# A two-layer hybrid decoder trunk on one core: another order of the first loads, transposes and products

## The chip, the cores and the metric

The kernel runs on one core of a Trainium2 chip. The core has five engines that run side by side and wait for each other through semaphores: TensorE (PE, with its weight loads PEld) multiplies matrices and transposes blocks, VectorE (DVE) and ScalarE (ACT) work on elements, GpSimd (POOL) does small odd jobs, and SyncE (SP) mainly issues transfers. ScalarE and GpSimd can issue transfers too. The metric is the device time of one execution in microseconds (us), the median of several runs.

## The reference, cut to what matters

The program computes two decoder layers for 256 tokens of width 2048, in float32. Layer 0 mixes tokens with a causal softmax attention of 16 heads with forget gates, layer 1 with three dilated windows of 8 heads. Before each mixer and each MLP stands an RMS norm, and all results are added to one residual stream:

```python
def reference(x, fox_w_in, ...):
    for i in range(DEPTH):
        h = rms_norm(x, mix_norm_g[i])
        if i % N_MIXERS == 0:
            mix = fox_attention(h, fox_w_in[j], fox_b_f[j], fox_q_gain[j], fox_k_gain[j], fox_w_out[j])
        else:
            mix = dilated_attention(h, dil_w_in[j], dil_q_gain[j], dil_k_gain[j], dil_w_out[j])
        x = x + mix
        h = rms_norm(x, mlp_norm_g[i])
        x = x + sq_relu_mlp(h, mlp_w_up[i], mlp_w_down[i])
```

The change touches the beginning of layer 0: the load of `x`, its first norm and the products of the normed `x` with `fox_w_in`, whose columns are queries, keys, values and 16 gate columns. `fox_w_in` is 2048 x 6160.

## The kernel before

**Products.** Every large product has 2048 rows of contraction, cut into 16 steps of 128 rows (`KC`), and 512 columns (`NC`). To keep float32 accuracy with a single-pass format, both operands are split into a high and a low part in `float32r`, and each step makes three matmuls for each of the two token blocks: high by high, high by low, low by high (lines 339 to 341). A step is therefore six matmuls of 512 columns. The sums stand in two of four PSUM banks `acc` (`sums`, line 326) until a chain of smaller work has read them.

**Weights.** A list `plan` holds all weight tiles in order of use, each two row blocks of 128 by 512 columns, 512 KB. `load` brings the next one into one of five `raw` buffers, `split` casts it to `wh` on ScalarE (line 308) and subtracts to get `wl` on VectorE (line 309), five buffers each. In the steady state, a product that has used up a tile calls `split` for the tile five further on. When a tile is loaded, its transfer is issued on SP's queue, which is worked in order.

**The first norm.** `x` stands in four tiles `x0` to `x3` of 512 columns (both token blocks). The products need it transposed and scaled by the norm's gains: TensorE transposes blocks of 128 into PSUM (`ptx`, line 473, 32 of them), ScalarE scales and rounds to the high part (line 478), VectorE takes the low part (line 479); two steps of the contraction make a pair `hT`. The norm's factor `rstd` is applied after the products. It comes from the sums of squares (`junk`, line 489), which are done later. For the other three norms the same turn is made by VectorE in 32x32 blocks, written to DRAM with four transfers a tile and read back with one (`transposed_by_dma`, line 429).

**The order of work.** The order is written out by a small planner, `Jobs`. Each chain of small work is a generator that yields a number of steps to wait, or a key that another chain has to set. Each contraction step calls `jobs.tick()`. The scheduler below it keeps this order as priority on each engine and moves an instruction back where its inputs come later by its own estimate. `behind(...)` fixes that what follows is queued behind given instructions of the same engine; it is an order and not a wait.

**The start.** `warm` makes ScalarE load its table for Exp; eight transposes of `ident` run on TensorE (`wake`, line 116). `load_x(0)` and the first weight tile go out in halves on SP's and ScalarE's queues. The gains of the first norm come through GpSimd's queue (line 141), are transposed on TensorE and copied on VectorE (`gained`). The next seven transfers are held until then: `hold` (line 265) writes one column of each target tile on VectorE behind `gained`, and the transfer has to wait for that write.

```python
    for what in (load, lambda: load_x(1), load, lambda: load_x(2), load, lambda: load_x(3), load):
        what()
        issued["held"] = []
```

Then the products follow, for each of four head groups `j`: queries, keys, values. For `j == 0` the gates (`gate`, 32 matmuls into `pf`) stand between queries and keys.

**After the products.** `qk_chain` (line 512) squares the sums, takes the norm of each head, scales, turns the tiles in 32x32 blocks, writes them to DRAM on SP's queue and reads them back on GpSimd's (line 544), then scales and splits them. `fox_head` (line 705) waits for queries, keys, gate and mask, and makes the scores `sc_f` (line 623). `make_sel` (line 745) builds a selection matrix on GpSimd through a tile `self` (lines 747 and 749). These chains share five buffers with the tag `w`: squares, scaled queries and keys, `self`, `junk` and turned tiles.

`in_pair` (line 353), used so far at the beginning of the later layers' parts, runs two products in turn: the first 12 steps of both (`CUT`), then the last 4 of both.

Of the kernel before, what the change touches and what calls it, by code (L numbers as in the profile page):

```python
# [38 lines left out]
CUT = 12  # L39

# [48 lines left out]
def trunk(ctx: ExitStack, tc, x, fox_w_in, fox_b_f, fox_q_gain, fox_k_gain, fox_w_out, dil_w_in,  # L89
# [17 lines left out]
    nc.scalar.activation(warm, warm, AF.Exp)  # L107
# [3 lines left out]
    nc.gpsimd.memset(mhalf, -0.5)  # L111


    spare = ps_sc.tile([P, P], F32, tag="sc", name="spare")

    def wake(times):
        for _ in range(times):
            nc.tensor.transpose(spare, ident, ident)

    wake(8)  # L120
# [20 lines left out]
    mix_rows = gain_rows("g_mix", [mix_norm_g.rearrange(per_chunk, p=P)], nc.gpsimd)  # L141
# [79 lines left out]
    def add_pair(*chunks):  # L221

        for rows in ((0, CUT * P), (CUT * P, D)):
            for w, cols in chunks:
                add(w, rows, cols)
# [6 lines left out]
    for j in range(4):  # L232
        for part in range(3):
            add(fox_w_in[0], (0, D), [(part * D + j * NC, NC)])
# [39 lines left out]
    raws, splits = [], []  # L274

    def load():
# [6 lines left out]
        for c, width in cols:  # L283
            src = w[r:r + RAW_SUB * P, c:c + width].rearrange("(c p) n -> p c n", p=P)
            if i:
                with hold(t[:, 0, 0:1]):
                    issued["load"] = nc.sync.dma_start(t[:, :, at:at + width], src)
            else:

                for part, queue in enumerate((nc.sync, nc.scalar)):  # L290
                    queue.dma_start(t[:, part, at:at + width], src[:, part, :])
            at += width
# [3 lines left out]
    def split():  # L296
# [9 lines left out]
        with behind(*([issued["gained"]] if i == 0 else issued.get("n0", []) if i < 2 * W_BUFS else [])):  # L306
            for part in ([slice(0, 1), slice(1, 2)] if i < 1 else [slice(0, W_SUB)]):
                issued["cast"] = nc.scalar.copy(hi[:, part, :], raw[:, part, :])  # L308
                issued["cut"] = nc.vector.tensor_sub(lo[:, part, :], raw[:, part, :], hi[:, part, :].bitcast(F32))  # L309
        splits.append((hi, lo))  # L310
        state["split"] += 1
# [17 lines left out]
    def product_steps(acc, keys, lhs, steps):  # L329

        for k in steps:
# [4 lines left out]
            for t in range(NT):  # L336
                tok = slice(t * P, (t + 1) * P)
                first, last = k == 0, k == KC - 1
                nc.tensor.matmul(acc[t], ah[:, tok], hi, start=first, stop=False)  # L339
                nc.tensor.matmul(acc[t], ah[:, tok], lo, start=False, stop=False)  # L340
                issued["product"] = nc.tensor.matmul(acc[t], al[:, tok], hi, start=False, stop=last)  # L341
            if i == W_SUB - 1:
                used[0] += 1
                split()
# [8 lines left out]
    def in_pair(new, steps, posts):  # L353
# [75 lines left out]
    def transposed_by_dma(tag, col, n):  # L429
# [31 lines left out]
    def norm_chain(tag, col, n, ssp, wait, later):  # L461
        yield wait
        if tag != "n0":
            yield from transposed_by_dma(tag, col, n)
        else:
            for half in range(2):
# [9 lines left out]
                for i in range(2):  # L476
                    gc = gain[:, col + pr * 2 + i:col + pr * 2 + i + 1]
                    on_act = nc.scalar.activation(both[:, i, 0, :], pt[:, i, :], AF.Copy, scale=gc)
                    on_dve = nc.vector.scalar_tensor_tensor(both[:, i, 1, :], pt[:, i, :], gc,
                                                            both[:, i, 0, :].bitcast(F32), ALU.mult, ALU.subtract)  # L480
# [429 lines left out]
    first = normed("n0", 0, lambda n: (0, 2, 6, 10)[n], lambda n: (13, 11, 9, 7)[n])  # L910

    def load_x(n):
        for t in range(NT) if n == 0 else [slice(0, NT)]:
            with hold(xt[n][:, 0, 0:1]):
                queue = nc.scalar if t == 1 else nc.sync
                issued["load"] = queue.dma_start(xt[n][:, t, :], xv[:, t, n * NC:(n + 1) * NC])

    def rest():
        while state["split"] - used[0] < W_BUFS:
            split()  # L920
            yield 1

    load_x(0)
    load()
    gained = gain_columns("g_mix", mix_rows, 0)

    issued["gained"] = gained
    issued["held"] = True
    for what in (load, lambda: load_x(1), load, lambda: load_x(2), load, lambda: load_x(3), load):
        what()  # L930
        issued["held"] = []
    del issued["held"]
# [11 lines left out]
    for j in range(4):  # L944
        sel = make_sel(j)
# [3 lines left out]
        product(keys_h(tag), lhs_h(tag), lambda acc: qk_chain(  # L949
            acc, tag, ("fq", j), [(0, 2, FOX_G, qT[0]), (2 * P, 2, FOX_G, qT[1])]))  # L950
        if j == 0:
            jobs.need("wf")
            gate(tag)
        product(keys_h(tag), lhs_h(tag), lambda acc: qk_chain(
            acc, tag, ("fk", j), [(0, 2, FOX_G + 1, kT[0]), (2 * P, 2, FOX_G + 1, kT[1])]))
# [46 lines left out]
```

## Time and profile before

| What | Value |
|---|---|
| median of 3 runs | 2161.55 us (2160.7 to 2162.31) |
| profiled execution, own time | 2161.91 us |
| its span | 2160.2 us |
| TensorE busy | 2147.8 us (99%), 11208 instructions |
| VectorE, ScalarE, GpSimd busy | 1397.9, 1105.9, 74.1 us |
| DMA | 459.34 MB, 213 GB/s in the mean |
| first product matmul | 8.53 us after the span's start |

The span goes from the first to the last profiled instruction; the execution's own time holds what lies around it as well. The profile names an instruction by line, engine, what it writes and what it reads. Idle time of an engine is put down to whatever released it. Busy matmuls are pipelined, so TensorE's pace is read from the distance of their starts. In rows of stretches the columns are the stretch, its length, busy time and count of PE, PEld, DVE, ACT and POOL, the granted clock, the DMA engines' share and GB/s.

### The profile page before, as it was taken

To read this page: it belongs to the slowest core of one execution; us is meant where nothing else is said; L and a number is where in the kernel's file an instruction comes from. 1 tells how busy PE (TensorE), PEld (TensorE's weight loads), DVE (VectorE), ACT (ScalarE), POOL (GpSimd) and SP (SyncE) were. 2 spreads that over 40 slices of the span, in tenths; PEclk is the share of its full clock that TensorE was granted. 3 is DMA by queue.
4 is the path that set the end of the run, shared out by engine and by line. 5 is a ranking of instruction groups with operands and counts; after the bars stand their busy time and mean duration, and the time that the engine had idled before them with its cause. 6 is when DMAs were issued, how large, how long until landed. Compare 5 with 4: busy or idle time off the path is not lost.

```text
span 2160.2 us, 30057 instructions
## 1 busy us (share of the span) xinstructions
PE 2147.8 (99%) x11208; PEld 1912.6 (89%) x11208; DVE 1397.9 (65%) x1862; ACT 1105.9 (51%) x1545; POOL 74.1 (3%) x92
## 2 busy tenths in 40 slices
PE   9999999999999999999999999999999999999999
PEld 7888888988998998998888888888988988988988
DVE  6777787765655565566668777676655655655664
ACT  6565655644544454455555565546544543544442
POOL 1111000000000000000011010100000000000000
PEclk9999999999999999999999999999999999999999
DMA  7676667766666666667776776758666666666664
GB/s 251 220 225 196 224 201 233 248 203 204 199 203 205 200 201 204 203 199 241 244 242 207 232 226 195 259 177 275 215 204 201 200 204 204 198 203 204 202 210 144
DMA packets 292354, 459.34 MB, mean 213 GB/s; under 512 B 21944, under 2 KB 104432, under 8 KB 292208
## 3 DMA queue, kind: packets, MB, share of 16 engines
q1 hardware_dynamic: 288416, 446.27, 66.1%
q0 software_dynamic: 3232, 10.50, 1.4%
q8 instruction: 87, 1.43, 0.3%
q10 hardware_dynamic: 560, 0.66, 0.1%
q14 instruction: 59, 0.48, 0.1%
HBM read 438.48 MB, written 18.87 MB: 212 GB/s over the span
## 4 chain that ended last, share of the span: by engine, by line
PE 92%; DVE 3%; DMA 2%; issue 1%; ACT 1%; POOL 0%; SPq 0%; DVEq 0%; ACTq 0%; POOLq 0%
PE acc L340 19%; PE acc L341 19%; PE acc L339 19%; PE up_n1a_acc L403 5%; PE up_n3a_acc L403 5%; PE up_n3a_sc L403 3%; PE up_n1a_tp L403 3%; PE up_n1a_sc L403 3%; PE up_n3a_tp L403 3%; PE up_n3a_acc L407 3%; PE up_n1a_acc L407 3%; DMA raw<-in_dil_w_in_dram 2%; DVE wl L309 1%; PE up_n3a_tp L407 1%; PE up_n1a_sc L407 1%; PE up_n1a_tp L407 1%
## 5 line engine op out<-in xcount | busy, mean ns | idle before, releaser
L309 DVE TENSOR_TENSOR wl<-raw,wh 128x1024 fp32r<-128x1024 f32 (+1 forms) x801 | 975.0, 1221 | 686.7 <-ACT wh L308 681.0
L308 ACT CAST wh<-raw 128x1024 fp32r<-128x1024 f32 (+1 forms) x801 | 837.7, 1048 | 931.7 <-PE acc L341 567.4
L339 PE MATMUL acc<-wh,hT_n 128*128 128x512 f32 x896 | 343.0, 384 | 0.5 <-ACT wh L308 0.5
L340 PE MATMUL acc<-wl,hT_n 128*128 128x512 f32 x896 | 339.9, 379 | 0.1
L341 PE MATMUL acc<-wh,hT_n 128*128 128x512 f32 x896 | 339.5, 379 | 0.0
L339 PE MATMUL acc<-wh,aTh_n1a 128*128 128x512 f32 x512 | 194.0, 379 | 0.0
L340 PE MATMUL acc<-wl,aTh_n1a 128*128 128x512 f32 x512 | 194.0, 379 | 0.0
L341 PE MATMUL acc<-wh,aTl_n1a 128*128 128x512 f32 x512 | 194.0, 379 | 0.0
L341 PEld LDWEIGHTS acc<-wh,hT_n 128*128 128x128 f32 x896 | 169.3, 189 | 24.1
L339 PEld LDWEIGHTS acc<-wh,hT_n 128*128 128x128 f32 x896 | 169.6, 189 | 23.4 <-ACT wh L308 0.9
L340 PEld LDWEIGHTS acc<-wl,hT_n 128*128 128x128 f32 x896 | 169.8, 190 | 22.6 <-DVE wl L309 0.4
L339 PE MATMUL acc<-wh,aTh_n3a 128*128 128x512 f32 x480 | 181.9, 379 | 0.0
L340 PE MATMUL acc<-wl,aTh_n3a 128*128 128x512 f32 x480 | 181.9, 379 | 0.0
L341 PE MATMUL acc<-wh,aTl_n3a 128*128 128x512 f32 x480 | 181.9, 379 | 0.0
L403 PE MATMUL up_n1a_acc<-hT_n,wh 128*128 128x512 f32 x512 | 181.6, 382 | 0.0
L403 PE MATMUL up_n3a_acc<-hT_n,wh 128*128 128x512 f32 x512 | 181.6, 382 | 0.0
L407 PE MATMUL up_n1a_acc<-hT_n,wl 128*128 128x256 f32 x512 | 139.6, 273 | 0.0
L407 PE MATMUL up_n3a_acc<-hT_n,wl 128*128 128x256 f32 x512 | 139.6, 273 | 0.0
L341 PEld LDWEIGHTS acc<-wh,aTl_n1a 128*128 128x128 f32 x512 | 96.8, 189 | 13.8
L340 PEld LDWEIGHTS acc<-wl,aTh_n1a 128*128 128x128 f32 x512 | 96.8, 189 | 13.7
L339 PEld LDWEIGHTS acc<-wh,aTh_n1a 128*128 128x128 f32 x512 | 96.8, 189 | 13.6
L403 PEld LDWEIGHTS up_n3a_acc<-hT_n,wh 128*128 128x128 f32 x512 | 96.8, 189 | 13.5
(725 smaller groups left out, 3202.3 us busy)
## 6 DMA issues: line engine op xcount, KB each, us to landing
raw<-in_mlp_w_up_dram SPq DMA_DIRECT2D x256, 512.0 KB, 4.1
raw<-in_mlp_w_down_dram SPq DMA_DIRECT2D x256, 512.0 KB, 4.2
raw<-in_dil_w_in_dram SPq DMA_DIRECT2D x192, 256.0 KB, 4.6
raw<-in_fox_w_in_dram SPq DMA_DIRECT2D x95, 512.0 KB, 4.1
raw<-in_fox_w_out_dram SPq DMA_DIRECT2D x32, 512.0 KB, 4.3
raw<-in_dil_w_in_dram SPq DMA_DIRECT2D x32, 512.0 KB, 4.4
raw<-in_dil_w_out_dram SPq DMA_DIRECT2D x32, 512.0 KB, 4.4
blocks_n<-turned_n SPq DMA_DIRECT2D x96, 64.0 KB, 2.4
```

The source lines that it names most:

```text
L308: issued["cast"] = nc.scalar.copy(hi[:, part, :], raw[:, part, :])
L309: issued["cut"] = nc.vector.tensor_sub(lo[:, part, :], raw[:, part, :], hi[:, part, :].bitcast(F32))
L339: nc.tensor.matmul(acc[t], ah[:, tok], hi, start=first, stop=False)
L340: nc.tensor.matmul(acc[t], ah[:, tok], lo, start=False, stop=False)
L341: issued["product"] = nc.tensor.matmul(acc[t], al[:, tok], hi, start=False, stop=last)
L403: issued["product"] = nc.tensor.matmul(banks[b], hi[:, i, col], in_turn(tokens.rearrange("p x s -> p (x s)"), P // 2), start=first, stop=last)
L407: nc.tensor.matmul(banks[b][:, 0:S], lo[:, i, col], in_turn(tokens[:, 0, :], P // 2), start=False, stop=False)
```

## The change

- The gains of the first norm are issued by ScalarE's queue instead of GpSimd's. The table load for Exp follows behind ScalarE's second transfer.
- `wake` runs float32r matmuls of 512 columns on a tile of zeros (a buffer of tag `w`) instead of transposes of `ident`: six at first, and two behind the first transposes.
- The first transfers are half of `x0` (256 columns, both token blocks), the first row block of weight tile 0 on ScalarE's queue, the second on SP's, the other half of `x0`, then weight tile 1.
- Six more transfers (`x1`, tiles 2, 3, 4, `x2`, `x3`) each wait for a fill of their whole target tile by GpSimd; the fills are queued one behind the other.
- The first split is made in two row blocks; the second one is queued behind the first pair of hT. The hT operations and the next splits are queued behind each other in the written order, and `rest` makes its first split one step later.
- Queries and keys of group 0 are made with `in_pair`, cut at 8 steps; the gates stand between their two last parts, and the first `make_sel` behind the pair. The weight plan follows that order.
- `x2` and `x3` are transposed like in the later norms, through DRAM; the block writes go by SP's queue and the read by GpSimd's. The due times in steps of the four parts change.

```diff
+FIRST_CUT = 8
...
-    nc.scalar.activation(warm, warm, AF.Exp)
...
-    nc.gpsimd.memset(mhalf, -0.5)
-    spare = ps_sc.tile([P, P], F32, tag="sc", name="spare")
+    ready = nc.gpsimd.memset(mhalf, -0.5)
+    spare = ps_sc.tile([P, NC], F32, tag="sc", name="spare")
+    zeros = work.tile([P, NC], F32R, tag="w", name="zeros", bufs=5)
+    nc.vector.memset(zeros.bitcast(F32), 0.0)
     def wake(times):
         for _ in range(times):
-            nc.tensor.transpose(spare, ident, ident)
-    wake(8)
+            nc.tensor.matmul(spare, zeros[:, 0:P], zeros, start=True, stop=True)
+    wake(6)
...
-    mix_rows = gain_rows("g_mix", [mix_norm_g.rearrange(per_chunk, p=P)], nc.gpsimd)
+    mix_rows = gain_rows("g_mix", [mix_norm_g.rearrange(per_chunk, p=P)], nc.scalar)
...
     for j in range(4):
-        for part in range(3):
-            add(fox_w_in[0], (0, D), [(part * D + j * NC, NC)])
+        chunks = [(fox_w_in[0], [(part * D + j * NC, NC)]) for part in range(3)]
+        if j == 0:
+            add_pair(*chunks[0:2], cut=FIRST_CUT)
+        for w, cols in chunks[2 if j == 0 else 0:]:
+            add(w, (0, D), cols)
...
-    def hold(first):
+    def hold(whole):
         if "held" not in issued:
             return ExitStack()
-        with behind(issued["gained"]):
-            nc.vector.memset(first, 0.0)
-        return behind(*([issued["load"]] if issued["held"] == [] else []))
+        with behind(*issued["held"]):
+            issued["held"] = [nc.gpsimd.memset(whole, 0.0)]
+        return behind(issued["load"])
...
-        with behind(*([issued["gained"]] if i == 0 else issued.get("n0", []) if i < 2 * W_BUFS else [])):
-            for part in ([slice(0, 1), slice(1, 2)] if i < 1 else [slice(0, W_SUB)]):
-                issued["cast"] = nc.scalar.copy(hi[:, part, :], raw[:, part, :])
-                issued["cut"] = nc.vector.tensor_sub(lo[:, part, :], raw[:, part, :], hi[:, part, :].bitcast(F32))
+        with behind(*(issued.get("n0", []) if i < 2 * W_BUFS else [])):
+            issued["cast"] = nc.scalar.copy(hi, raw)
+            issued["cut"] = nc.vector.tensor_sub(lo, raw, hi.bitcast(F32))
         splits.append((hi, lo))
+        cuts.append(issued["cut"])
...
-                nc.tensor.matmul(acc[t], ah[:, tok], hi, start=first, stop=False)
+                with behind(*([issued["product"]] if first and 0 < used[0] < W_BUFS else [])):
+                    nc.tensor.matmul(acc[t], ah[:, tok], hi, start=first, stop=False)
...
-                split()
+                if state["split"] >= W_BUFS:
+                    split()
...
-    def in_pair(new, steps, posts):
+    def in_pair(new, steps, posts, cut=CUT, between=lambda: None):
         banks = []
         for n in range(2):
             banks.append(new(n))
-            steps(banks[n], range(CUT))
+            steps(banks[n], range(cut))
         for n in range(2):
-            steps(banks[n], range(CUT, KC))
+            steps(banks[n], range(cut, KC))
             jobs.spawn(posts[n](banks[n]))
+            if n == 0:
+                between()
...
-    def transposed_by_dma(tag, col, n):
+    def transposed_by_dma(tag, col, n, queue, steps, *order):
...
-            nc.vector.transpose(tile_.rearrange("p (j b r) -> p b j r", j=4, b=4),
-                                xt[n][:, t, :].rearrange("p (b j c) -> p b j c", j=4, c=32))
+            with behind(*order):
+                nc.vector.transpose(tile_.rearrange("p (j b r) -> p b j r", j=4, b=4),
+                                    xt[n][:, t, :].rearrange("p (b j c) -> p b j c", j=4, c=32))
...
-            nc.sync.dma_start(tile_, blocks.rearrange("j c i x -> (j c) (i x)"))
+            queue.dma_start(tile_, blocks.rearrange("j c i x -> (j c) (i x)"))
             tiles.append(tile_)
-        yield 9
+        yield steps
...
-            yield from transposed_by_dma(tag, col, n)
+            yield from transposed_by_dma(tag, col, n, nc.sync, 9)
+        elif n > 1:
+            yield from transposed_by_dma(tag, col, n, nc.gpsimd, 9 + n, cuts[n + 2], issued["n0"][1])
...
+                    with behind(*issued.get(tag, [])):
+                        on_act = nc.scalar.activation(both[:, i, 0, :], pt[:, i, :], AF.Copy, scale=gc)
+                        on_dve = nc.vector.scalar_tensor_tensor(both[:, i, 1, :], pt[:, i, :], gc,
+                                                                both[:, i, 0, :].bitcast(F32), ALU.mult, ALU.subtract)
+                    issued[tag] = on_act, on_dve
...
-    first = normed("n0", 0, lambda n: (0, 2, 6, 10)[n], lambda n: (13, 11, 9, 7)[n])
+    first = normed("n0", 0, lambda n: (0, 2, 4, 5)[n], lambda n: (8, 9, 4, 2)[n])
...
     def rest():
+        yield 1
         while state["split"] - used[0] < W_BUFS:
...
+    nc.sync.dma_start(*halves_x[0])
+    with behind(nc.scalar.dma_start(first_raw[:, 0, :], first_w[:, 0, :])):
+        nc.scalar.activation(warm, warm, AF.Exp)
+    with behind(nc.sync.dma_start(first_raw[:, 1, :], first_w[:, 1, :])):
+        issued["load"] = nc.sync.dma_start(*halves_x[1])
...
+    with behind(issued["load"]):
+        load()
+    issued["held"] = [ready]
+    for what in (lambda: load_x(1), load, load, load, lambda: load_x(2), lambda: load_x(3)):
         what()
...
+    split_row_block(0)
     jobs.spawn(first(0))
     with behind(issued["transposed"]):
-        wake(3)
-    split()
-    for n in range(1, NX):
+        wake(2)
+    with behind(*issued["n0"]):
+        split_row_block(1)
...
+    jobs.spawn(first(1))
+    jobs.spawn(rest())
+    for n in range(2, NX):
         jobs.spawn(first(n))
-    jobs.spawn(rest())
...
-        sel = make_sel(j)
+        sel = make_sel(j) if j else None
...
+        if j == 0:
+            in_pair(lambda n: sums(), lambda acc, ks: product_steps(acc, keys_h(tag), lhs_h(tag), ks),
+                    [q_post, k_post], FIRST_CUT, gates)
+            sel = make_sel(j)
+        else:
+            product(keys_h(tag), lhs_h(tag), q_post)
+            product(keys_h(tag), lhs_h(tag), k_post)
```

`gates` is the former call of `gate`, `q_post` and `k_post` are the former `qk_chain` calls, and `split_row_block` casts and subtracts one row block of tile 0 behind `gained`.

More of the change, by code (lines that the diff above doesn't have):

```diff
@@ L219, in add, with add_pair @@
             plan.append((w, r, cols))
-    def add_pair(*chunks):
-        for rows in ((0, CUT * P), (CUT * P, D)):
+    def add_pair(*chunks, cut=CUT):
+        for rows in ((0, cut * P), (cut * P, D)):
             for w, cols in chunks:
@@ L284, in load @@
             src = w[r:r + RAW_SUB * P, c:c + width].rearrange("(c p) n -> p c n", p=P)
[L285 to L291, printed above, removed]
+            with hold(t):
+                issued["load"] = nc.sync.dma_start(t[:, :, at:at + width], src)
             at += width
@@ L907, in normed @@
         return lambda n: norm_chain(tag, col, n, ssp, wait(n), later(n))
-    first = normed("n0", 0, lambda n: (0, 2, 6, 10)[n], lambda n: (13, 11, 9, 7)[n])
+    first = normed("n0", 0, lambda n: (0, 2, 4, 5)[n], lambda n: (8, 9, 4, 2)[n])
     def load_x(n):
[L913 to L916, printed above, removed]
+        with hold(xt[n]):
+            issued["load"] = nc.sync.dma_start(xt[n], xv[:, :, n * NC:(n + 1) * NC])
     def rest():
+        yield 1
         while state["split"] - used[0] < W_BUFS:
```

36 lines of the change are left out of this document (21 added, 15 removed).

## The prediction

> **What bounds the kernel now.** I read the page's first part, then the list of who waited for whom on TensorE, then the busy time by stretches, and last the timeline of the first 20 us.
>
> ```profile
> span 2160.2 us, 30057 instructions
> ...
> PE 2147.8 (99%) x11208; PEld 1912.6 (89%) x11208; DVE 1397.9 (65%) x1862; ACT 1105.9 (51%) x1545; POOL 74.1 (3%) x92
> ```
> ```profile
> PE spare L118 <- POOL ident masks.py:199: 2.5, 1, 2.5
> PE ps_g_mix L137 <- DMA g_mix<-in_mix_norm_g_dram: 2.1, 1, 2.1
> ...
> PE sc_f L623 <- ACT fkT_0h L560: 1.1, 1, 1.1
> ...
> PE acc L339 <- ACT wh L308: 0.5, 1, 0.5
> ```
> ```profile
> 0.00:8.53 8.53, 3.88 (x16) 3.10 (x16) 2.00 (x12) 3.10 (x5) 4.89 (x16) 1.00 0.46 128
> 8.53:15.58 7.05, 6.44 (x31) 5.04 (x31) 3.54 (x7) 3.77 (x7) 0.00 (x0) 1.00 0.99 325
> 15.58:23.02 7.44, 7.44 (x41) 6.55 (x40) 5.50 (x8) 5.02 (x10) 0.00 (x0) 1.00 1.05 389
> ...
> 85.25:87.75 2.50, 1.26 (x7) 0.86 (x6) 1.99 (x3) 2.50 (x6) 0.00 (x0) 1.00 0.20 46
> ```
> ```profile
> 8.53:15.58 7.05, 5.62 (x18) 3.60 (x19) 0.00 (x0) 0.00 (x0) 1.00 0.99 325
> 15.58:23.02 7.44, 7.05 (x30) 5.61 (x31) 0.00 (x0) 0.00 (x0) 1.00 1.05 389
> ```
> ```profile
> 15.39 0.44 PE ptx_n L473 x4
> 15.83 0.22 PE acc L339
> ```
>
> The reader is to see that TensorE is the bound nearly everywhere. The four waits shown, 6.2 us together (2.5, 2.1, 1.1 and 0.5), all lie in the first 88 us. The third fence is busy time by stretches (PE, weight loads, DVE, ACT, POOL), the fourth the same for the matrix products into `acc` alone, the fifth two rows of the chain that ended last. A product matmul costs 0.22 us, a step of the contraction has six of them (1.3 us), a transpose of a 128x128 block costs 0.44/4 = 0.11 us. So 8.53 to 15.58 holds three steps, 18 x 0.216 = 3.9 us, and 12 transposes, 1.3 us: 5.2 us of work in 7.05 us, 1.9 us lost. The next 7.44 us hold five steps, 6.5 us, and 8 transposes, 0.9 us: nothing is lost there. What can be won is therefore the start (8.53 us before the first product), the 1.9 us after it, PE work that is taken away, and the wait of the first attention head at 85 us. The rest of the kernel only shifts.
>
> **The change part by part.** The start of before, from the timeline:
>
> ```profile
> 0.81 0.42 ACTq L916 DMA_DIRECT2D x<-in_x_dram  x1
> 1.42 0.66 POOL L130 DMA_DIRECT2D g_mix<-in_mix_norm_g_dram  x1 [0.33 <-issue]
> 2.43 0.54 POOL L747 MEMSET self<- 128x512 f32 x1
> 6.19 1.14 ACT L308 CAST wh<-raw 128x512 fp32r<-128x512 f32 x2 [3.43 <-DMA raw<-in_fox_w_in_dram]
> 6.62 0.31 PE L137 MATMUL ps_g_mix<-ident,g_mix 32*128 32x32 f32 x1 [2.11 <-DMA g_mix<-in_mix_norm_g_dram]
> 6.86 1.11 PE L473 MATMUL ptx_n<-ident,x 128*128 128x128 f32 x4
> 7.20 0.38 SPq L287 DMA_DIRECT2D raw<-in_fox_w_in_dram  x1
> 8.01 0.47 ACT L478 ACTIVATE hT_n<-ptx_n,gain 128x256 fp32r<-128x256 f32 x1 [0.68 <-PE ptx_n L473]
> 8.53 0.80 PE L339 MATMUL acc<-wh,hT_n 128*128 128x512 f32 x1
> 9.03 0.47 ACT L478 ACTIVATE hT_n<-ptx_n,gain 128x256 fp32r<-128x256 f32 x1 [0.55 <-DVE hT_n L479]
> 9.54 0.48 DVE L479 SCALAR_TENSOR_TENSOR hT_n<-ptx_n,gain,hT_n 128x256 fp32r<-128x256 f32 x1 [0.54 <-ACT hT_n L478]
> 9.97 0.38 PE L340 MATMUL acc<-wl,hT_n 128*128 128x512 f32 x1
> 10.19 0.59 PE L341 MATMUL acc<-wh,hT_n 128*128 128x512 f32 x2
> 11.91 1.04 ACT L308 CAST wh<-raw 128x1024 fp32r<-128x1024 f32 x1 [0.17 <-DMA raw<-in_fox_w_in_dram]
> 12.98 1.23 DVE L309 TENSOR_TENSOR wl<-raw,wh 128x1024 fp32r<-128x1024 f32 x1 [0.73 <-ACT wh L308]
> 15.65 1.23 DVE L309 TENSOR_TENSOR wl<-raw,wh 128x1024 fp32r<-128x1024 f32 x1 [0.48 <-ACT wh L308]
> 18.35 1.22 DVE L309 TENSOR_TENSOR wl<-raw,wh 128x1024 fp32r<-128x1024 f32 x1 [0.69 <-ACT wh L308]
> ```
> ```profile
> x<-in_x_dram ACTq DMA_DIRECT2D x1, 256.0 KB, 4.0
> turned_n<-blocks_n SPq DMA_DIRECT2D x24, 256.0 KB, 2.9
> qn_('fq', 0)_1_576<-blocks_('fq', 0)_1_586 POOLq DMA_DIRECT2D x1, 256.0 KB, 5.8
> ```
>
> *First loads and gains.* In before the gains, issued by GpSimd at 1.42, hold the transposes until 6.62. Now ScalarE issues them first, at 0.81, and they are 16 KB: they cannot be later than the 256 KB which the same queue brought in 4.0 us, at 4.8. The half of x that the first two steps need is 256 KB at the head of SP's queue: 4.8 us by the same row. Row block 0 of the weights stands second on ScalarE's queue behind 16 KB. It lands between 4.8 and the 6.2 us at which before had all of its first 1 MB; I take 5.1. Its cast is 1.14/2 = 0.57 us, so it is done at 5.7. From the first transpose to the first product before took 8.53 - 6.86 = 1.67 us, hence the first product starts at 4.85 + 1.67 = 6.5 us (7.2 if the row block comes at 6.2; 6.1 if the transposes run at full pace).
>
> *From the first product to the fourth step.* The second row block is now cast behind the second hT operation of ScalarE. By the rows 8.53, 9.03 and 9.54, that operation begins 0.5 us after the first product and its VectorE partner ends at +1.5; the cast ends at +1.55, the subtraction of 0.69 at +2.2, while the first step's six matmuls end at +1.3 to +2.0. Then four transposes (+0.45), hT on ScalarE, VectorE, ScalarE (three times 0.5), which ends at about +3.8, then raw1's cast, which stands behind them in the new order: 1.04, to +4.8. Step 2 starts there, its low part after the subtraction of 1.23 at +6.0, and step 3 starts at +6.5, with all 16 remaining transposes done: 13.0 us. Before started that step at 15.58 with the same 16 done. Gain 2.6 us. In before, raw1, issued at 7.20 behind the gains, was the late one (cast at 11.91, the wait of 0.5); now it is sent right after x's second half without a wait, is there by about 8 us, and ScalarE's order is what comes last.
>
> *Transposes of x2 and x3.* 16 of 32 leave TensorE: 16 x 0.11 = 1.7 us. The first two products in pair give them time: x2 is needed only at the ninth step of the first product, after 16 steps of work, at about 13.0 + 13 x 1.3 = 29.8 us.
>
> *Idle float32r matmuls.* Six of 512 columns on zeros from about 1.3 us, two more behind the first transposes. They run beside the loads and cost nothing. The first four products of before stood nearly 0.5 us apart (8.53 to 9.97), the next two 0.22: at least 0.8 us lost at half pace, though the granted clock reads 1.00 throughout. The wait on `ident` disappears too, and nothing hangs on it. If TensorE is at full pace from 4.8 us on, 1.3 us are won (0.4 on the transposes, so that the first product comes at 6.1, and 0.8 or a little more on the products); if the pace comes as late as before, nothing. I take 0.4. [...]
>
> *Fills on GpSimd.* Six fills of 128x1024, 1.1 us each (0.54 for 512 columns), so loads go out about as fast as 390 GB/s can take them (512 KB in 1.35 us); raw1 to raw4, x2 and x3 then land one after the other until about 15 us, 5 us ahead of before. TensorE eats one in 2.6 us. Cost nothing; were the loads late, each would cost its own delay, as raw1's did.
>
> *The pace of the splits.* Before, subtraction followed subtraction in 2.7 us (12.98, 15.65, 18.35) with a pair of hT in between, and TensorE needs 2.6 for two steps. With the new order behind hT, a chain by hand gives 3.25 us (1.23 + 0.5 + 0.5 + 0.5 + 1.04, less some overlap): two times 0.7. Between 0 and 1.4 I take 0.4, nearer to the measured pace.
>
> *x2 through DRAM.* Its turning on VectorE stands behind raw4's subtraction, at about 20 us by the same count.
>
> ```profile
> 51.62 1.80 SPq L543 DMA_DIRECT2D blocks_('fq', 0)_0_579<-sq_('fq', 0)_0_525  x4
> 53.52 1.85 SPq L543 DMA_DIRECT2D blocks_('fq', 0)_1_586<-sq_('fq', 0)_1_527  x4
> 57.40 0.55 POOL L544 DMA_DIRECT2D qn_('fq', 0)_1_576<-blocks_('fq', 0)_1_586  x1 [1.46 <-DMA blocks_('fq', 0)_1_586<-sq_('fq', 0)_1_527]
> 73.19 0.53 POOL L747 MEMSET self<- 128x512 f32 x1 [8.08 <-DVE fqT_1l L562]
> 73.80 2.54 POOL L749 TENSOR_SCALAR_AFFINE_SELECT self<-self 128x512 f32<-128x512 f32 x2
> 76.29 0.60 POOL L544 DMA_DIRECT2D qn_('fk', 0)_0_771<-blocks_('fk', 0)_0_777  x1
> ```
>
> The same path for the queries took 51.62 to 57.40 + 5.8 = 63.2, 11.6 us. From 20.7 that is 32.3, against a need at 29.8 for the first token half and 30.5 for the second: up to 1.8 us of wait. With SP's 2.9 us for the same read it would be 29.4 and no wait. The eight block writes, 3.65 us of SP's time for each x tile, stand ahead of raw loads, which have 5 us in hand; GpSimd's queue is empty there. Half of the measured excess, lessened by products that can run on the first half: 0.5.
>
> *The head's wait at 85 us* (1.1 us, 1.3 with its latency). TensorE waits for the keys, whose read GpSimd issued at 76.29 behind `self` of the next group, which had waited 8 us for the last reader of a query tile. Counted in steps of the job list, the query chain started at step 19, where `rstd` is due in before, and the key chain at 32; now the query product ends at step 24 and the key product still at 32, so the queries are five steps later against the keys, and `make_sel(0)` stands between them. If `self` of the next group falls behind the keys' reads, 3.1 us are won and the wait is gone; if the queries' later release holds the keys, it grows (rival 3). I take -0.6, half of the wait.
>
> Sum: -2.6 - 1.7 - 0.4 + 0.4 + 0.5 - 0.6 = -4.4 us on 2160.2 of span. The profiled run's own time was 2161.91, the median 2161.55, so they stand within 0.4 us; 2161.55 - 4.4 = 2157.1, by 0.20%. 0.2%, 4.3 us, is about what a measurement of this kernel can tell from no change.
>
> **The rivals.**
>
> 1. *The start is won and the splits and x2 give it back.* Both upper ends: +1.0 for the pace and +1.3 for x2, the head's wait unchanged, +0.6: -1.5, so 2160.0. For it: the new order on ScalarE, and 5.8 us for GpSimd's reads. Against it: the 2.7 us pace. [...]
>
> 2. *The start doesn't come earlier.* Row block 0 shares the 16 DMA engines with x's halves and raw1 and comes with the whole first megabyte at 6.2: first product 7.2, step 3 at 13.7, and no pace won. That leaves -1.9 - 1.7 + 0.9 - 0.6 = -3.3: 2158.2.
>
> 3. *The keys come late for the first heads, and it ends slower.* The `w` tiles are five. The query chain holds three of them; `self` takes the next one free and 3.1 us of GpSimd; the keys' tiles follow. With the queries released 5 steps (6.5 us) later against the keys' product, the keys are 6.5 + 3.1 = 9.6 us later and the wait of 1.3 becomes 10.9: -4.4 + 0.6 + 9.6 = +5.8, 2167.3. It is slower from 3.8 us of growth on, by over 0.2% from 8.1 on. Against it: the written order of TensorE's work can put products ahead of that head.
>
> **How the numbers follow.** The sum as it stands, or better, 0.50: faster by over 0.2%, predicted 2156.7, midway between the sum (2157.1) and what full pace from the start gives (2156.2). Rival 1, 0.28, and rival 2, 0.10, both within 0.2%. Rival 3, 0.12, of which 0.10 slower by over 0.2% and 0.02 within. So 0.50, 0.40, 0.10. Range: below, all good ends (full pace -1.3 in place of -0.4, pace and x2 free, -0.9, no head wait, -0.7): -6.9, 2154.6. Above, rivals 1 and 2 whole and the small case of rival 3: 2161.8.
>
> **What would show it.** The first product at 6.1 to 7.2 us (8.53 before); matmuls 0.22 apart from the first step on if the pace is full; step 3 at 13.0; 16 `ptx` transposes in place of 32; no stretch with idle TensorE at 30 us; the wait of `sc_f` near 81 us gone or as before. Wrong if the first product isn't ahead of 7.5 us, if TensorE waits over 2 us for hT of x2, or if a wait of `sc_f` above 3 us stands in the list.

## The result and the profile after

The changed kernel takes 2182.22 us (median; 2182.05 to 2183.47) against 2161.55 us: a ratio of 1.0098, 95% interval 1.0087 to 1.0108. It is 20.7 us slower. The forecast was 2156.7 us, with a range up to 2161.8 us.

The first rows of the page, and then the list of who waited for whom on TensorE (us in total, times, longest), of the changed kernel:

```profile
span 2180.5 us, 30075 instructions
...
PE 2152.5 (99%) x11189; PEld 1914.7 (88%) x11189; DVE 1402.4 (64%) x1868; ACT 1107.5 (51%) x1553; POOL 80.4 (4%) x101
```
```profile
PE acc L341 <- ACT hT_n L459: 8.8, 1, 8.8
PE sc_f L633 <- ACT fkT_0h L570: 3.4, 1, 3.4
PE ps_g_qk L139 <- DMA g_qk<-in_dil_k_gain_dram: 3.0, 1, 3.0
PE sc_f L630 <- ACT fkT_0w L563: 2.2, 1, 2.2
PE acc L341 <- ACT hT_n L487: 1.7, 1, 1.7
```

The wait on `g_mix` is gone. In its place stand longer ones, and all three signs of being wrong that the prediction named are there: a first product behind 7.5 us, over 2 us of wait for hT of `x2`, and over 3 us for `sc_f`. Line 459 is hT made from `x2` and `x3`, the parts that come back from DRAM. It costs most. Lines 630 and 633 are the scores of the first heads, 5.6 us where before had 1.1. `g_qk` is a small constant that TensorE transposes, in its written order, ahead of that hT product. TensorE's busy time rose too, by 4.7 us, although there are 19 instructions fewer. The stretches show why. Columns: stretch, length, busy time and count of PE, PEld, DVE, ACT and POOL, granted clock, DMA share, GB/s.

```profile
5.90:7.62 1.72, 0.05 (x1) 0.00 (x0) 0.39 (x1) 0.99 (x2) 0.88 (x1) 1.00 1.01 369
7.62:8.50 0.88, 0.88 (x3) 0.51 (x4) 0.69 (x2) 0.15 (x1) 0.00 (x0) 1.00 1.06 410
8.50:10.00 1.50, 1.50 (x4) 1.17 (x5) 1.12 (x2) 0.83 (x2) 0.00 (x0) 0.50 1.06 408
10.00:11.50 1.50, 1.50 (x7) 1.26 (x6) 0.06 (x1) 0.26 (x1) 0.00 (x0) 0.50 1.05 385
...
34.00:38.30 4.30, 0.25 (x2) 0.22 (x2) 0.56 (x2) 0.00 (x0) 2.18 (x7) 1.00 0.55 168
38.30:47.20 8.90, 0.16 (x1) 0.05 (x1) 4.50 (x11) 5.21 (x11) 0.06 (x1) 0.55 0.99 347
47.20:50.00 2.80, 2.77 (x7) 2.20 (x8) 1.94 (x7) 2.80 (x8) 0.00 (x0) 0.50 1.03 349
50.00:52.40 2.40, 2.40 (x7) 1.95 (x6) 2.40 (x6) 2.26 (x8) 0.00 (x0) 0.50 0.49 158
53.00:60.00 7.00, 7.00 (x34) 6.14 (x33) 4.11 (x10) 6.42 (x15) 0.53 (x1) 1.00 0.56 169
```

TensorE stands nearly still from 33.8 to 47.2 us, and after it the clock is granted at 0.50 for 5.2 us: seven matmuls in 2.8 us, where full pace makes 34 in 7.0.

The starts of the contraction steps, counted from 0 and read from the timelines, place the loss (us after the span's start):

| step | before | changed | later by |
|---|---|---|---|
| 0 (first product) | 8.53 | 7.62 | -0.9 |
| 3 | 15.59 | 16.31 | +0.7 |
| 15 | 32.97 | 32.51 | -0.5 |
| 24 (behind the gates in both) | 49.37 | 64.10 | +14.7 |
| 50 | 83.97 | 99.09 | +15.1 |
| 54 (behind the first head) | 91.64 | 112.70 | +21.1 |

So the loss has two places: 15.2 us between steps 15 and 24, and 5.9 us at the first heads. From there on the two kernels run in parallel, and the spans end 20.3 us apart.

**The first place.** Three queues meet there. SP's queue, then ScalarE, then the product that waited (timeline of the changed kernel):

```profile
22.91 10.61 SPq L445 DMA_DIRECT2D blocks_n<-turned_n  x16
33.57 0.48 SPq L166 DMA_DIRECT2D bf<-in_fox_b_f_dram  x1
34.09 0.32 SPq L132 DMA_DIRECT2D g_qk<-in_fox_q_gain_dram  x1
...
36.29 27.36 SPq L292 DMA_DIRECT2D raw<-in_fox_w_in_dram  x13
```
```profile
25.37 1.05 ACT L308 CAST wh<-raw 128x1024 fp32r<-128x1024 f32 x1 [1.72 <-DMA raw<-in_fox_w_in_dram]
...
41.63 1.04 ACT L308 CAST wh<-raw 128x1024 fp32r<-128x1024 f32 x1 [15.21 <-DMA raw<-in_fox_w_in_dram]
...
45.24 1.03 ACT L308 CAST wh<-raw 128x1024 fp32r<-128x1024 f32 x1
...
46.80 0.39 ACT L459 ACTIVATE hT_n<-turned_n,gain 128x128 fp32r<-128x128 f32 x1
```
```profile
47.23 0.79 PE L341 MATMUL acc<-wh,hT_n 128*128 128x512 f32 x1 [8.77 <-ACT hT_n L459]
```

The 16 block writes of `x2` and `x3` hold SP's queue from 22.91 to 33.52 us, and the small constants stand behind them. Fourteen of the writes take 0.4 to 0.5 us each to issue, the first and the fourth 2.1 and 1.6 us. The next weight tile, the tenth, is issued only at 36.29. Its cast on ScalarE starts at 41.63, after 15.21 us in which ScalarE did nothing. The casts of the tenth, eleventh and twelfth tile stand ahead of hT in ScalarE's written order, so hT starts at 46.80, although its data were read from 29.5 and 31.5 us on, 3.8 us in the median to the landing. TensorE needed only the ninth tile for this product, and that was cast at 25.37.

**The second place.** GpSimd before the first heads, changed kernel:

```profile
84.78 0.52 POOL L757 MEMSET self<- 128x512 f32 x1 [3.71 <-ACT fqT_1w L563]
...
92.84 0.53 POOL L757 MEMSET self<- 128x512 f32 x1 [6.06 <-DVE fqT_1l L572]
93.43 2.55 POOL L759 TENSOR_SCALAR_AFFINE_SELECT self<-self 128x512 f32<-128x512 f32 x2
95.93 0.59 POOL L554 DMA_DIRECT2D qn_('fk', 0)_0_778<-blocks_('fk', 0)_0_784  x1
```

The read of the keys stands behind two `self` now, group 0's and group 1's. Each had to wait until a query tile with the tag `w` was read for the last time.

### The profile page after: what moved, and what is told of

Same layout as the page of the kernel before. It is cut to its first block, busy times and chain, and to the rows that moved or that the text cites. A ratio compares the mean times of both kernels' runs of the same rounds, so it can differ in the third digit from the quotient of the medians.

```text
span 2180.5 us, 30075 instructions
## 1 busy us (share of the span) xinstructions
PE 2152.5 (99%) x11189; PEld 1914.7 (88%) x11189; DVE 1402.4 (64%) x1868; ACT 1107.5 (51%) x1553; POOL 80.4 (4%) x101
## 4 chain that ended last, share of the span: by engine, by line
PE 93%; DMA 3%; DVE 2%; ACT 1%; issue 1%; SPq 1%; POOL 0%; ACTq 0%; DVEq 0%; POOLq 0%
PE acc L341 19%; PE acc L343 19%; PE acc L342 19%; PE up_n1a_acc L408 5%; PE up_n3a_acc L408 5%; PE up_n1a_sc L408 3%; PE up_n1a_tp L408 3%; PE up_n3a_tp L408 3%; PE up_n3a_sc L408 3%; PE up_n3a_acc L412 3%; PE up_n1a_acc L412 3%; DVE wl L309 1%; PE up_n3a_sc L412 1%; PE up_n3a_tp L412 1%; PE up_n1a_tp L412 1%; PE up_n1a_sc L412 1%
## 5 line engine op out<-in xcount | busy, mean ns | idle before, releaser
L309 DVE TENSOR_TENSOR wl<-raw,wh 128x1024 fp32r<-128x1024 f32 x799 | 974.0, 1223 | 687.9 <-ACT wh L308 684.9
L308 ACT CAST wh<-raw 128x1024 fp32r<-128x1024 f32 x799 | 836.4, 1049 | 943.7 <-PE acc L343 563.4
```

Of the source, the lines that this page charges most:

```text
L308: issued["cast"] = nc.scalar.copy(hi, raw)
L309: issued["cut"] = nc.vector.tensor_sub(lo, raw, hi.bitcast(F32))
```

## The experiments

Each ratio compares with runs of the kernel before on the same chip: 2160.94 us for e1 to e4, 2161.59 us for e5, e6, e7 and e9, 2161.26 us for e10 and e11. What a run wins against the changed kernel is told as the difference of the two medians, 2182.22 us less its own; the changed kernel ran on another chip, and the medians of the kernel before differ by up to 0.65 us between the chips, so such a difference is no more exact than that.

**x2 and x3 turned by TensorE again** (label e1_pe_turn), the rest as changed:

```diff
-        elif n > 1:
-            yield from transposed_by_dma(tag, col, n, nc.gpsimd, 9 + n, cuts[n + 2], issued["n0"][1])
```

> The changed kernel with x2 and x3 transposed by TensorE again (16 transposes, 1.7 us), all else as changed. Theory A: the wait at 34 to 47 us comes from the block writes of x2 and x3 on SP's queue, which stand ahead of the loads of weight tiles 9 to 11, and from ScalarE's order, which puts hT of x2 behind the casts of those tiles. Without the writes the wait (12.8 us) and the half pace after it (2.5 us) are gone: 2182.2 - 15.3 + 1.7 = about 2168.6, tile 9 issued near 23 us. Rival B, the pairing itself starves the products: no change, 2180 or more.

Measured 2167.23 us, ratio 1.0027 [1.0017, 1.0037]. The longest waits of TensorE:

```profile
PE sc_f L631 <- ACT fkT_0h L568: 4.0, 2, 3.5
...
PE sc_f L628 <- ACT fkT_0w L561: 1.3, 1, 1.3
```

15.0 us come back with the detour through DRAM, as much as the first place holds in the table. The wait for hT and that for `g_qk` are both gone; the heads' wait stays.

**The block writes on GpSimd's queue** (e2_writes_gpsimd), the rest as changed:

```diff
-                nc.sync.dma_start(blocks[:, :, i, :].rearrange("j c x -> c j x"),
+                (queue if tag == "n0" else nc.sync).dma_start(blocks[:, :, i, :].rearrange("j c x -> c j x"),
```

> The changed kernel with the sixteen block writes of x2 and x3 on GpSimd's queue, ahead of its reads, so that SP sends weight tile 9 right after the gains. Theory A: tile 9 is issued near 25 us instead of 36.3, its cast is no longer late, and hT of x2 waits only for its own data, which land at 35 to 38 us: 8 to 11 us are won, 2171 to 2174. Rival C, the way of x2 through DRAM is itself what comes last: no gain, 2180 to 2184.

Measured 2176.55 us, ratio 1.0071 [1.0056, 1.0086]. SP's queue, then GpSimd's:

```profile
25.85 19.41 SPq L292 DMA_DIRECT2D raw<-in_fox_w_in_dram  x9
```
```profile
35.36 0.57 POOL L447 DMA_DIRECT2D turned_n<-blocks_n  x1 [4.54 <-DMA blocks_n<-turned_n]
35.92 2.18 POOL L445 DMA_DIRECT2D blocks_n<-turned_n  x4
42.28 0.57 POOL L447 DMA_DIRECT2D turned_n<-blocks_n  x1 [4.19 <-DMA blocks_n<-turned_n]
```

The tenth weight tile goes out at 25.85 in place of 36.29, and 5.7 us are won. That is less than the 8 to 11 expected. Writes and reads stand behind each other in GpSimd's queue now. Two of the four reads wait over 4 us for their writes, the others 1.9 and 1.0, and hT keeps 7.0 us of waits. The queue was moved, and the order inside it became the new bound.

**hT of x2 and x3 out of ScalarE's and VectorE's fixed order** (e5_free_order), the rest as changed:

```diff
-                    with behind(issued["cast"]):
+                    with behind(*([] if tag == "n0" else [issued["cast"]])):
...
-                    with behind(issued["cut"]):
+                    with behind(*([] if tag == "n0" else [issued["cut"]])):
```

> The changed kernel, in which hT of x2 and x3 is no longer queued behind the casts and subtractions of the weight tiles. SP's order stays as changed. Theory A has two halves: SP's queue makes tiles 9 to 11 late, and ScalarE's order makes hT of x2 wait for their casts. If the order is the larger half, the ninth step starts when the data of x2 have landed, near 36 to 37 us instead of 47.2, and TensorE then waits for tile 9 near 43 us: 7 to 10 us won, 2172 to 2175. If the late tiles alone count, nothing is won: 2181 to 2183. Rival C, x2's data come last: nothing won either, the ninth step stays near 47.

Measured 2174.24 us, ratio 1.0062 [1.0047, 1.0077]. ScalarE and TensorE:

```profile
33.25 1.28 ACT L459 ACTIVATE hT_n<-turned_n,gain 128x128 fp32r<-128x128 f32 x4 [6.66 <-DMA turned_n<-blocks_n]
35.51 0.69 ACT L459 ACTIVATE hT_n<-turned_n,gain 128x128 fp32r<-128x128 f32 x2 [0.97 <-DMA turned_n<-blocks_n]
```
```profile
35.96 0.48 PE L341 MATMUL acc<-wh,hT_n 128*128 128x512 f32 x1 [1.28 <-ACT hT_n L459]
```

8.0 us are won. Now hT waits for its data alone, at 33.25 and 35.51 us, and the wait for the data costs TensorE 1.3 us. The tenth weight tile still leaves at 36.31. It is cast at 43.36 and the step that uses it starts at 44.95; TensorE runs the gates in the meantime and waits 1.4 us for hT of `x3`. At step 24 the kernel is 3.9 us behind before, where the changed kernel is 14.7. Part of that gain is lost again: a new wait of 1.6 us ends at 75.57, for a value of the gates (`g_lf`), and the clock stands at 0.50 behind it, so that 8.3 us are missing at step 48. So the long wait is made of both: the late tile, and the order that carries its delay over to an hT that doesn't need it.

**The reads of x2 and x3 on SP's queue** (e10_read_sync), the rest as changed:

```diff
-            yield from transposed_by_dma(tag, col, n, nc.gpsimd, 9 + n, cuts[n + 2], issued["n0"][1])
+            yield from transposed_by_dma(tag, col, n, nc.sync, 9 + n, cuts[n + 2], issued["n0"][1])
```

> The changed kernel with one edit: the reads of x2 and x3 from DRAM are issued by SP instead of GpSimd. If GpSimd's slow reads (5.8 us against 2.9 us from SP) cause the wait at the seventeenth step, they end 2.9 us earlier and the time falls to 2178-2180 us. If SP's order causes it (weight tile 9 issued at 36.3 us, after the block writes and the constants), the two reads wait in that same queue for the writes to land and push tile 9 further back by 1 to 4 us: 2183-2186 us, a wait above 8.8 us.

Measured 2183.61 us, ratio 1.0105 [1.0091, 1.0118]. SP's queue and TensorE's waits:

```profile
38.95 0.35 SPq L447 DMA_DIRECT2D turned_n<-blocks_n  x1
...
40.05 26.72 SPq L292 DMA_DIRECT2D raw<-in_fox_w_in_dram  x13
```
```profile
PE acc L341 <- ACT hT_n L459: 8.3, 1, 8.3
PE ps_g_qk L139 <- DMA g_qk<-in_dil_k_gain_dram: 6.8, 1, 6.8
```

The rival "GpSimd's read is slow" forecast 2178 to 2180 us and falls. The edit also moved the reads themselves, though, the first two to 29.96 and 32.90 us from 29.54 and 31.45; e5_free_order says it more plainly, where the reads stay on GpSimd and the wait is 1.3 us. The reads go into the line that was too long already, and the tenth tile leaves 3.8 us later still. The wait for hT itself didn't grow as expected; the one for `g_qk`, which stands behind the reads in that queue, did, from 3.0 to 6.8 us.

**A buffer of its own for `self`** (e3_self_own), the rest as changed:

```diff
-        sf = work.tile([P, 4, P], F32, tag="w", name=f"self{j}", bufs=5)
+        sf = work.tile([P, 4, P], F32, tag="t2", name=f"self{j}")
```

> The changed kernel with the tile self in a buffer of its own (that of t2, free at that time) instead of one of the five w buffers. Theory D: the wait of the first head's scores (5.6 us in two parts, 1.1 before) comes from self taking w buffers and GpSimd's time ahead of the keys. GpSimd then makes both self tiles early and issues the keys' reads without them: qn of the keys about 6 us earlier against the end of the key product, wait 0 to 1.5 us, 2176 to 2178. Rival: the keys are late because the queries come late in the pair: 2181 to 2183. The wait at 34 to 47 us stays in either case.

Measured 2176.51 us, ratio 1.0074 [1.0059, 1.0089]. GpSimd and the waits:

```profile
90.50 0.58 POOL L554 DMA_DIRECT2D qn_('fk', 0)_0_778<-blocks_('fk', 0)_0_784  x1 [9.97 <-DVE fqT_0l L572]
```
```profile
PE sc_f L633 <- ACT fkT_0h L570: 3.0, 2, 1.8
```

The keys' read leaves 5.4 us earlier, and 5.7 us are won by the medians. No `self` stands in front any more; what remains is a wait for another `w` tile of the queries. The profiled run, at the slow end of its spread, still loses 2.4 us between steps 50 and 54, where the changed kernel loses 5.9.

**The pair alone, in the kernel before** (e4_pair_alone):

```diff
+FIRST_CUT = 8
...
-        for part in range(3):
-            add(fox_w_in[0], (0, D), [(part * D + j * NC, NC)])
+        chunks = [(fox_w_in[0], [(part * D + j * NC, NC)]) for part in range(3)]
+        if j == 0:
+            add_pair(*chunks[0:2], cut=FIRST_CUT)
+        for w, cols in chunks[2 if j == 0 else 0:]:
+            add(w, (0, D), cols)
...
+            in_pair(lambda n: sums(), lambda acc, ks: product_steps(acc, keys_h(tag), lhs_h(tag), ks),
+                    [q_post, k_post], FIRST_CUT, gates)
+            sel = make_sel(j)
```

> The kernel before with the pairing alone (plan order, cut at 8 steps, gates between, make_sel behind the pair); start, transposes and loads as before. Theory A: no wait at the ninth step, since all x is transposed by TensorE. Theory D: the first head waits 5 to 6 us instead of 1.1, so about 2166. Rival B, the pairing starves the products: a wait of 10 us or more behind step 16, 2175 or more. If neither: 2161 to 2162.

Measured 2166.42 us, ratio 1.0024 [1.0014, 1.0035]. GpSimd:

```profile
70.41 0.53 POOL L753 MEMSET self<- 128x512 f32 x1 [4.11 <-ACT fqT_1w L559]
...
78.47 0.53 POOL L753 MEMSET self<- 128x512 f32 x1 [6.06 <-DVE fqT_1l L568]
...
81.56 0.60 POOL L550 DMA_DIRECT2D qn_('fk', 0)_0_752<-blocks_('fk', 0)_0_758  x1
```

The pair brings the second place into a kernel with the old start: 5.5 us slower, the keys' read at 81.56 where before has 76.29, and the same two `self` ahead of it. No wait for hT appears. So the two places are independent.

**Both repairs together** (e6_pe_self): x2 and x3 turned by TensorE, and `self` in a buffer of its own; the two diffs above.

> The changed kernel with both cures: TensorE transposes x2 and x3, and self has a buffer of its own. Theories A and D add up: 2167.2 less the 4 to 5 us that the own buffer took from the first head, 2162 to 2164. If the pair holds the keys back by itself (queries due five steps later), 2165 to 2167.

Measured 2161.70 us, ratio 1.0005 [0.9996, 1.0014]. The heads' wait on TensorE:

```profile
PE sc_f L631 <- ACT fkT_0h L568: 1.5, 2, 1.0
```

Both long waits are gone, and with them the 20.7 us that the change cost. One by one the repairs won 15.0 and 5.7 us; against the kernel before on each run's own chip it is 14.4 and 5.1, so they add up to within about 1 us, and the exact 20.7 is partly luck. Seven of the ten values lie from 2160.4 to 2162.4 us and three from 2164.4 to 2167.0; one of the seven was profiled, so what the three lose isn't shown. What is left of the change, the new start and the pair with `self` apart, is worth nothing that can be told.

**The new start alone** (e7_start_alone): no pair, all turns on TensorE, `self` as before.

```diff
-        if j == 0:
-            add_pair(*chunks[0:2], cut=FIRST_CUT)
-        for w, cols in chunks[2 if j == 0 else 0:]:
+        for w, cols in chunks:
...
-        elif n > 1:
-            yield from transposed_by_dma(tag, col, n, nc.gpsimd, 9 + n, cuts[n + 2], issued["n0"][1])
...
-            in_pair(lambda n: sums(), lambda acc, ks: product_steps(acc, keys_h(tag), lhs_h(tag), ks),
-                    [q_post, k_post], FIRST_CUT, gates)
-            sel = make_sel(j)
+            gates()
+        product(keys_h(tag), lhs_h(tag), k_post)
```

> The changed start alone (gains by ScalarE, half of x first, fills by GpSimd, float32r matmuls on zeros, splits in their new order); queries, gates and keys one after the other as before, all x transposed by TensorE. The start won 0.9 us at the first product and 0 to 0.5 at the fourth step in the runs so far, and lost it by the ninth: 2160.5 to 2162 against 2160.9 of before. If the start were worth the 2.6 us that was forecast: 2158 to 2159.

Measured 2162.07 us, ratio 1.0003 [0.9994, 1.0012]. The profiled execution is the fastest of the ten (2160.11 us). Its first product starts at 7.54 us, 1.0 ahead of before. At step 3 it is 0.6 ahead, with 16 transposes made in both kernels, and at step 15, with all 32 made, 0.2. (The ninth step is level, +0.1 us, but four more transposes lie behind it than in before.) The splits took a part: TensorE waits 0.57 us for the cast of tile 1 and 0.56 us for its subtraction, 0.48 and 0.12 in before. VectorE's next subtractions:

```profile
12.36 1.22 DVE L307 TENSOR_TENSOR wl<-raw,wh 128x1024 fp32r<-128x1024 f32 x1 [0.45 <-ACT wh L306]
15.46 1.23 DVE L307 TENSOR_TENSOR wl<-raw,wh 128x1024 fp32r<-128x1024 f32 x1 [0.45 <-ACT wh L306]
```

They stand 3.1 us apart where before had 2.7, and two steps of TensorE need 2.6. Between steps 3 and 15 the list has no wait of TensorE above 0.1 us, so the 0.4 us lost there aren't put down to a cause.

**Gains first and `self` apart, in the kernel before** (e9_gains_self):

```diff
-    nc.scalar.activation(warm, warm, AF.Exp)
...
-    mix_rows = gain_rows("g_mix", [mix_norm_g.rearrange(per_chunk, p=P)], nc.gpsimd)
+    mix_rows = gain_rows("g_mix", [mix_norm_g.rearrange(per_chunk, p=P)], nc.scalar)
...
-        sf = work.tile([P, 4, P], F32, tag="w", name=f"self{j}", bufs=5)
+        sf = work.tile([P, 4, P], F32, tag="t2", name=f"self{j}")
...
+    with behind(issued["first"]):
+        nc.scalar.activation(warm, warm, AF.Exp)
```

> The kernel before with two small edits: the gains of the first norm go first on ScalarE's queue, with the Exp table behind its transfers, and self has the buffer of t2. The gains held the transposes until 6.6 us and the release of tile 1 until 7.2; by the changed kernel's trace they land at 3.6. First product at 6.7 to 7.2 us, tile 1 released at about 5.2, the wait for its cast gone: 2 to 2.7 us. The next group's self no longer stands ahead of the keys' reads on GpSimd (3.1 us), the wait of the first head is gone: 1.2 us. 2157 to 2158.5. If the first loads come last, not the gains: 2159.5 to 2160.

Measured 2159.36 us, ratio 0.9990 [0.9981, 0.9999], a little ahead of both kernels. The head's wait is gone from the list. The first product comes 1.0 us earlier, at 7.52, but its matmuls stand 0.43 us apart up to 11.8, and at step 15 0.2 us remain. That is short of the 2157 to 2158.5 us expected: with the gains out of the way the loads come last (TensorE waits 0.9 us for `x` until 5.86, and the first row block is cast at 5.60).

**The same with idle float32r matmuls** (e11_gains_self_idle), beside the diff above:

```diff
+    spare = ps_sc.tile([P, NC], F32, tag="sc", name="spare")
+    zeros = work.tile([P, NC], F32R, tag="w", name="zeros", bufs=5)
+    nc.vector.memset(zeros.bitcast(F32), 0.0)
...
-            nc.tensor.transpose(spare, ident, ident)
+            nc.tensor.matmul(spare, zeros[:, 0:P], zeros, start=True, stop=True)
-    wake(8)
+    wake(9)
```

> The kernel before with the gains first on ScalarE's queue, self in a buffer of its own, and idle float32r matmuls in place of the transposes of ident (nine, and three behind the first transposes). Alone the first two gave 2159.36 us, with matmuls 0.43 us apart from 7.5 to 11.8 us. If early activity brings full pace from the first product on, 1.3 to 2 us more are won: 2157.3-2158.1 us. If the idle wait for x still brings half pace, or the loads come last anyway: 2159-2160 us.

Measured 2158.23 us, ratio 0.9986 [0.9977, 0.9995]: the lowest median of all, just above the 2157.3 to 2158.1 us expected. TensorE:

```profile
6.46 0.93 PE L119 MATMUL spare<-zeros 128*128 128x512 f32 x3
7.80 0.48 PE L340 MATMUL acc<-wh,hT_n 128*128 128x512 f32 x1 [0.41 <-ACT hT_n L479]
8.12 0.38 PE L341 MATMUL acc<-wl,hT_n 128*128 128x512 f32 x1
8.55 0.48 PE L342 MATMUL acc<-wh,hT_n 128*128 128x512 f32 x1
8.87 0.38 PE L340 MATMUL acc<-wh,hT_n 128*128 128x512 f32 x1
9.09 0.38 PE L341 MATMUL acc<-wl,hT_n 128*128 128x512 f32 x1
```

Only 0.41 us are idle in front of the first product, and the matmuls stand 0.22 us apart from the fourth on. The first product comes later than in the run before (7.80), yet the start is 0.7 us ahead at step 15 (0.2 there). In the time, the intervals of these two runs overlap; that the idle matmuls win is shown by the trace and not by the medians.

## Why the prediction was wrong

- *x2 through DRAM* is the step that failed. It said +0.5 us, at most 1.8; the place cost 15.2. Its estimate of the data was fair: in e5_free_order hT of the first token half starts at 33.25 us, without a wait of TensorE, and that of the second at 35.51, with 1.3 us (forecast: all data by 32.3, up to 1.8 us of wait). The small wait is partly luck, since the need came at 33.9 and 34.5 us, 4 us later than forecast, as did the data by 3 us. What failed is the sentence on the block writes, that they "stand ahead of raw loads, which have 5 us in hand". The writes held SP's queue for 10.6 us, not 7.3, because two of the issues were slow. That isn't a wait for VectorE, which had turned `x2` and `x3` by 25.80. The issue right behind `wf` is slow in the kernel before as well (`bf`, 4.6 us) and in e1_pe_turn (3.0 us); why isn't shown. The constants stood behind them, so the tenth tile went out at 36.29 us, where e1_pe_turn, without those writes, had SP's queue clear for it at 25.57. And the prediction looked for who waits for the tile, but not for who stands behind its cast: it didn't go through ScalarE's written order, where hT follows the cast of a tile three further on. Idle time of TensorE is 3.0 + 1.1 + 8.8 = 12.9 us of the 15.2 (the 1.1 on `g_mlp`), the slow pace after it makes up the rest: two steps took 52.5 - 47.2 = 5.3 us in place of 2.6.
- *The head's wait at 85 us* was taken as -0.6 and cost +5.9: 4.5 us more of idle time, and the clock at 0.50 behind it (from 104.1 to 110.9 us). Rival 3 had it right in kind: the `w` buffers, `self` and the queries' later release. Its growth of 9.6 us was too large: `self` stood ahead of the keys' read in before too (73.19 to 76.29), so that its 3.1 us were counted twice, and the queries' release came 5.3 us later in e4_pair_alone (78.47), not 6.5; the keys' read moved by 5.3 us. That its 2167.3 us stands near the 2166.4 of the pair alone is partly chance. Its chance, 0.12, was too small: what stood against it, that products could be put ahead, rested on no row.
- *First loads and gains.* The gains and x's half came as forecast, but the first row block of the weights didn't. The profile of ScalarE has

```profile
6.58 0.62 ACT L956 CAST wh<-raw 128x512 fp32r<-128x512 f32 x1 [3.29 <-DMA raw<-in_fox_w_in_dram]
```

  where 5.1 us was taken for the landing, so the first product came at 7.62 us, past the 7.5 named as a sign of error. That is rival 2's mechanism, with its late row block.
- *From the first product to the fourth step* said 13.0 us for step 3; it was 16.3, and 15.6 before. The half pace (clock 0.50 from 8.5 to 11.9 us) and the later splits ate the gain: in e1_pe_turn, with the clock at 1.00 there, the step starts at 15.04.
- *Idle float32r matmuls* said -0.4. They did bring a faster pace early (the first four transposes took 0.86 us, 1.11 in before), and it was gone behind the wait of 1.7 us: the clock is 0.50 from 8.5 us on. In e1_pe_turn the transposes took 1.11 us too, but behind a wait of 1.1 us the clock stayed at 1.00.
- *The pace of the splits* said +0.4 of at most 1.4; the distance of 3.25 us worked out by hand was right (3.1 in e7_start_alone), and the cost was near: from step 3 to step 15 the changed kernel takes 16.2 us, of which its 72 matmuls are 15.5 and 0.7 is lost; before takes 17.4, of which 15.5 are matmuls, 1.7 are 16 transposes and 0.2 is lost.
- *Transposes of x2 and x3* did leave TensorE. Their 1.7 us are in the -0.5 at step 15, which without them would stand at +1.2.
- *Fills on GpSimd* cost nothing that shows.

Rival 1 named the places where the start would be given back, the splits and x2, and its upper end for x2 was 1.8 us. So no rival held the largest cost either, the one at the detour.

## What to carry to other kernels

Transfers hold up everything behind them in their issue queue, by the time that they take to issue (16 writes, 10.6 us) and by waiting for their producer (a read in e2_writes_gpsimd, 4.5 us): before moving work there, list what stands behind it up to the next large load, small constants among it, and then list what stands behind that load's consumer in the written order of its engine. A detour that takes 1.7 us of work from the bound engine is worth nothing if it joins such a chain. Where one pool of buffers serves several chains, work out who frees the buffer that each chain takes next, before two chains change places.

## What the runs showed of the hardware

The granted clock fell after quite short idle waits ahead of the first product. After 1.7 us (the changed kernel), 1.8 (e5_free_order), 2.0 (e3_self_own) and 2.2 (e10_read_sync) it stood at 0.50 about a microsecond after the first product at the latest, and came back 3.4 us later. After 1.0 (e6_pe_self), 1.1 (e1_pe_turn), 1.2 (e7_start_alone) and 1.3 us (e2_writes_gpsimd) it stayed at 1.00. Length isn't settled as the cause: the four kernels with the longer wait are also those whose transposes in front of it ran faster (four in 0.66 to 0.86 us, 1.11 in the others). Nor does length alone decide: in the kernel before, a wait of 2.1 us (until 6.62 us) left the granted clock at 1.00, though the first products behind it still started 0.43 us apart (9.12, 9.55 and 9.97 us).

GpSimd's reads were not as slow as rival 1 had it: 3.8 us in the median for `x2` and `x3` in the changed kernel, where 5.8 had been taken from the queries' read.
